# Two-layer encoder trunk: the order of products, SwiGLU transposes and token sums at the start of each FFN

## The chip, the core and the metric

The kernel runs on one core of one Trainium2 chip. The metric is the device time of one execution in microseconds (us); smaller is better. A kernel's time is the median of its runs. One further execution is taken with the hardware profiler; all rows below come from it. Engines are named as in the profile: PE (TensorE, matrix products), PEld (its weight loads), DVE (VectorE), ACT (ScalarE), POOL (GpSimd), SP (SyncE, which issues the DMAs).

## What is computed

A trunk of two layers over 256 tokens of width 1024, all in float32. Each layer is a half-step SwiGLU FFN, a token-mixing block and a second half-step FFN:

```python
def swiglu(h, w_up, w_down):
    a, b = jnp.split(h @ w_up, 2, axis=-1)
    return (jax.nn.silu(a) * b) @ w_down

for l in range(DEPTH):                      # 2
    h = rms_norm(x, ffn1_pre_g[l])
    x = x + 0.5 * rms_norm(swiglu(h, ffn1_w_up[l], ffn1_w_down[l]), ffn1_post_g[l])
    h = rms_norm(x, mix_pre_g[l])
    ...                                     # pooling, differential attention, cross-attention, gates
    x = x + rms_norm(merged @ w_out[l], mix_post_g[l])
    h = rms_norm(x, ffn2_pre_g[l])
    x = x + 0.5 * rms_norm(swiglu(h, ffn2_w_up[l], ffn2_w_down[l]), ffn2_post_g[l])
```

D_FF is 2816, so w_up is 1024 x 5632 and w_down 2816 x 1024. There are four FFNs in all.

## The kernel before

**Precision.** Every float32 operand of a product is split into a high part in the PE's fast format (ACT copies it, tiles `wh` for weights) and the remainder (DVE subtracts, `wl`). A product is three matrix products: high by high, high by low, low by high (`mm3`, L229). Weights come from memory in units of 128 x 2048 (`raw`, 1 MB, five buffers) and are split by `split_unit` (L113) into five pairs of `wh`/`wl` buffers; a sixth unit waits until the PE has done with the first.

**Tokens.** The 256 tokens are two halves c = 0 and 1 of 128 rows. The normed activations lie transposed and split in `xhl`. The hidden width is cut into 11 blocks p of 256 columns. The up product of block p and half c (`up`, L344) uses two weight units (upper and lower half of the 1024 inputs), has 24 matmuls of 512 columns, and fills one PSUM bank: 256 columns of a, 256 of b. Below it is called product pc: 00, 10, 01 and so on, the block first. `swiglu` (L334) then has ACT take the Silu of a into `sg` (L340) and DVE multiply by b into `hn` (L341), both SBUF tiles of the eight-buffer pool `s2`. Its result must be transposed for the down product: `turned` (L320) puts a closure on the list `pending`; when `flush` (L307) calls it, the PE makes two 128 x 128 transposes into a bank `mb` (L325), and ACT and DVE split that into `hid[p]` (L164, L165). Below the transposes of block p and half c are t00, t10 and so on.

**PSUM.** Eight banks: four accumulators `acc`, two `ma` for products, two `mb` for transposes. `down(p)` (L311) adds block p's down product into the four accumulators, which are taken at the first of them, `down(0)`, and kept to the FFN's end. The stage ahead uses the same four for its own result; `post_norm` (L217) reads them last.

**Start of an FFN.** The first FFN (the kernel's first stage) starts with `up_first` and is left out here. The three later ones make, in this order, products 00, 10, 01, 11 (L446 to L448), each in an `ma` bank, and after each product's matmuls `flush()` issues every transpose that is pending. So the PE's order is 00, 10, t00, 01, t10, 11, t01. The second half's normed tokens are only just being made when the FFN starts: their eight transposes (L207) are placed by hand after the 37th of these matmuls (`issue_after(late, done[T_UP])`, T_UP = 36), that is in the middle of product 10. ACT and DVE then split them into `xhl` (L164, L165), and ACT also copies them unsplit into four `s2` tiles, `kept` (L212). From these `token_sums` (L372) forms four sums and differences on DVE (L375 to L378) and splits each (ACT and DVE, L164 and L165) for the products of `group`.

**The rest of an FFN.** Blocks follow a list, `PLAN`: for the three later FFNs `u2 d0 g3 d1 d2 u5 d3 g6 d4 d5 u8 d6 g9 d7`. `u` is `up_both` (two products of one block), `d` is `down`, and `g` is `group` (L382), which makes two blocks at once by seven products of half the size from sums of weight units (DVE adds whole `raw` tiles, L364, then they are split like others) and sums of tokens. Its second product, into an `mb` bank, is the first that reads the token sums.

**Order on the engines.** A planner takes the instructions in program order as priority and lays out each engine's own order ahead of time, by what it expects to be ready; where its own estimate says that an operand is late, it takes later instructions first. Each engine then executes its list in order and waits where an operand is late.

Of the kernel before, what the change touches and what calls it, by code (L numbers as in the profile page):

```python
# [51 lines left out]
def encoder_kernel(ctx, tc, x_d, xt_d, mem_d, memt_d, pos_d, w_d, gains_d, cols_d, lamv_d, poolw_d, cst_d, out_d):  # L52
# [24 lines left out]
    def t2(shape=(P, 512), dt=F32):  # L77
        return s2.tile(list(shape), dt, name="s2")
# [48 lines left out]
    def next_unit():  # L127
        parts = 4 if fine[0] > 0 else 2
        fine[0] -= 1
        return split_unit(next_raw(), parts)  # L130
# [6 lines left out]
    def issue_after(late, early):  # L137
        for i in late:
            tc.add_manual_dep(i.ins, early.ins.name, mybir.DependencyInfo(mybir.DependencyClass.NoSync, mybir.DependencyReason.DATA),
                              reason="issue order")  # L140

    def in_order(ins):
        for early, late in zip(ins, ins[1:]):
            issue_after([late], early)
# [6 lines left out]
    def rstd_of(halves, fold=1.0, between=None, into=None, listed=False):  # L151
        s, sq = sm(2), []
        for i, h in enumerate(halves):
            junk = small.tile([P, 512], BF16, name="junk", bufs=2)
            sq.append(nc.scalar.activation(out=junk, in_=h, func=AF.Square, scale=fold / 32.0, accum_out=s[:, i:i + 1]))  # L155
        v = sm(1)
        var = nc.vector.tensor_scalar(out=v, in0=s[:, 0:1], scalar1=s[:, 1:2], scalar2=fold * fold * EPS, op0=ALU.add, op1=ALU.add)  # L157
        if between:
            between(var)
        r = rsqrt(v, 1, into)  # L160
        return (var, sq) if listed else r

    def split(ps, h, l):
        high = nc.scalar.copy(out=h, in_=ps)  # L164
        return high, nc.vector.tensor_tensor(out=l, in0=ps, in1=h.bitcast(F32), op=ALU.subtract)  # L165

    def halves(t):
        return [t[:, 0:512], t[:, 512:1024]]
# [95 lines left out]
    def form_b2(out, lo, hi, c, xx):  # L264
        return mm3(out, half_b(lo, 0, c, xx) + half_b(hi, 1, c, xx))
# [31 lines left out]
    def ffn(i, xx, late, kept, g_post, finish, ahead, raw_rstd=None):  # L297
# [9 lines left out]
        def flush(leave=0):  # L307
            while len(pending) > leave:
                pending.pop(0)()
# [24 lines left out]
        def swiglu(p, c, ps):  # L334
            sg, hn = t2((P, S)), t2((P, S))
            if raw_rstd:
                nc.scalar.activation(out=sg, in_=ps[:, 0:S], func=AF.Silu, scale=raw_rstd[c])
                nc.vector.scalar_tensor_tensor(out=hn, in0=ps[:, S:2 * S], scalar=raw_rstd[c], in1=sg, op0=ALU.mult, op1=ALU.mult)
            else:
                nc.scalar.activation(out=sg, in_=ps[:, 0:S], func=AF.Silu)  # L340
                nc.vector.tensor_tensor(out=hn, in0=ps[:, S:2 * S], in1=sg, op=ALU.mult)  # L341
            turned(hn, c, [p])

        def up(p, c, ws, bank=ma_bank):  # L344
            ps = bank()
            now = form_b2(ps, ws[0], ws[1], c, xx)
            flush()
            swiglu(p, c, ps)
            return now

        def up_both(p):
            ws = (next_unit(), next_unit())
            for c in range(2):
                up(p, c, ws)

        def product(out, at, w, first=True, last=True):
            wv = [t.rearrange("p (k m) -> p k m", k=4) for t in w]
# [14 lines left out]
        def token_sums():  # L372
            a11, a12, a21, a22 = (kept[c, b] for c in range(2) for b in range(2))
            s1 = t2()
            nc.vector.tensor_tensor(out=s1, in0=a22, in1=a21, op=ALU.subtract)  # L375
            nc.vector.tensor_tensor(out=a21, in0=a11, in1=a21, op=ALU.subtract)
            nc.vector.scalar_tensor_tensor(out=a11, in0=s1, scalar=-1.0, in1=a11, op0=ALU.mult, op1=ALU.subtract)
            nc.vector.scalar_tensor_tensor(out=a12, in0=a11, scalar=-1.0, in1=a12, op0=ALU.mult, op1=ALU.subtract)  # L378
            for j, t in enumerate((s1, a11, a21, a12)):
                split(t.rearrange("p (k t) -> p k t", t=P), sums[:, 0, 4 * j:4 * j + 4, :], sums[:, 1, 4 * j:4 * j + 4, :])  # L380
# [42 lines left out]
        def up_first(p, ws):  # L423
            banks = [ma_bank(), ma_bank()]
            for j, w in enumerate(ws):
                for c in range(2):
                    mm3(banks[c], half_b(w, j, c, xx), j == 0, j == 1)
            for c in range(2):
                swiglu(p, c, banks[c])

        if raw_rstd:
            ws = [(next_unit(), next_unit())]
            hs, ls = first_high, first_low
            (ha, la), (hb, lb), (hc, lc), (hd, ld) = (zip(*late[c, b]) for b in range(2) for c in range(2))
            in_order([*ha, *hs[0:4], *hb, *hc, hs[4], hs[5], *hd, *hs[6:8]])
            in_order([*la, *ls[0:4], *lb, *lc, ls[4], ls[5], *ld, *ls[6:8]])
            ws.append((next_unit(), next_unit()))
            for c in range(2):
                rstd_of(halves(x[c]), 1.0, None, raw_rstd[c])
            up_first(0, ws[0])  # L440
            for c in range(2):
                up(1, c, ws[1], acc_bank)
        else:
            ws = [(next_unit(), next_unit()) for _ in range(2)]
            done = []
            for c in range(2):  # L446
                for p in range(2):
                    done += up(p, c, ws[p])  # L448
            issue_after(late, done[T_UP])
            token_sums()  # L450
        for n, (what, p) in enumerate(PLAN[bool(kept)]):
            if what == "d":
                down(p)
            elif what == "u":
                up_both(p)
            else:
                group(p)
            if not kept and n == 5:
                ahead()
# [403 lines left out]
    kept = None  # L863
    for i, (kind, l, row) in enumerate(stages):
        nx = {}

        def finish(c):
            if i + 1 == len(stages):
                for b in range(2):
                    fs = slice(b * 512, (b + 1) * 512)  # L870
                    nc.sync.dma_start(out=out_d[c * P:(c + 1) * P, fs], in_=x[c][:, fs])
                return []
            if c == 0:
                nx["xx"] = xt_pair()
                nx["kept"] = {} if stages[i + 1][0] == "ffn" else None
                nx["g"] = gain(stages[i + 1][1] * 10 + stages[i + 1][2])
            return pre_norm(c, halves(x[c]), nx["g"], nx["xx"], nx["kept"])()

        if kind == "ffn":
            def ahead():  # L880
                if i == 0:
                    setup()
                    mem_scale()
                if row == 0:
                    nx["mem"] = mem_gain(l)

            late = ffn(i, cur, late, kept, gain(l * 10 + row + 1), finish, ahead, [rst[:, c:c + 1] for c in range(2)] if i == 0 else None)
        else:
            late = mix(l, cur, late, mem, finish)
        cur, mem, kept = nx.get("xx"), nx.get("mem"), nx.get("kept")  # L890
# [117 lines left out]
```

## Time and profile before

| | us |
|---|---|
| median of 3 runs | 1126.62 |
| the runs | 1125.84, 1126.62, 1129.25 |
| the profiled execution, device time | 1127.05 |
| its span, first to last instruction | 1124.9 |
| PE busy | 1109.0 (99%) |
| DVE busy | 893.5 (79%) |
| ACT busy | 651.9 (58%) |
| granted PE clock, mean | 0.997 |

The profiled execution's device time is 2.15 us over its span, and 0.43 us over the median. A granted clock of 1.00 is 2.4 GHz, of 0.50 is 1.2 GHz. The three FFNs in question start at about 385, 566 and 940 us of the span. A matmul's row in a timeline shows a modelled duration, which overlaps with the next one's start; how often matmuls start tells the PE's real pace.

### The profile page before, as it was taken

How to read it: one execution, taken by the hardware profiler on the slowest of the kernel's cores; microseconds unless marked ns; L12 is line 12 of the kernel's file. 1: busy time of each engine (PE TensorE's matmuls, PEld its weight loads, DVE VectorE, ACT ScalarE, POOL GpSimd, SP SyncE). 2: the span in 40 equal slices, each digit the busy share in tenths (PEclk: the TensorE clock that was granted, in tenths of full speed). 3: DMA queues.
4: the chain of work that ended last, by engine and by line, in shares of the span. 5: the costliest groups of instructions: out<-in, count | busy, mean ns of one | idle time of the engine just before them, and what ended most of it. 6: DMA issues, size and time to landing. Idle time of an engine off the chain costs nothing.

```text
span 1124.9 us, 13897 instructions
## 1 busy us (share of the span) xinstructions
PE 1109.0 (99%) x5247; PEld 913.2 (81%) x5247; DVE 893.5 (79%) x1215; ACT 651.9 (58%) x1082; POOL 26.1 (2%) x37
## 2 busy tenths in 40 slices
PE   9999999999999999999999999999999999999997
PEld 6888888888888878888878888878887887888886
DVE  6767456657758889999989999995776687999994
ACT  7657355556575557475575664755566546574561
POOL 0000000000000100000000000010000001000000
PEclk9999999999999999999999999999999999999999
DMA  9965643554553554573851835666455634263831
GB/s 342 388 229 225 219 152 117 192 220 150 206 206 132 195 179 148 190 264 136 310 190 73 299 135 202 219 240 218 160 175 191 244 149 169 75 245 135 293 112 38
DMA packets 35489, 218.27 MB, mean 194 GB/s; under 512 B 4192, under 2 KB 4448, under 8 KB 11232
## 3 DMA queue, kind: packets, MB, share of 16 engines
q1 hardware_dynamic: 35424, 217.40, 53.4%
q8 instruction: 41, 0.67, 0.2%
q14 instruction: 24, 0.20, 0.1%
HBM read 216.33 MB, written 1.05 MB: 193 GB/s over the span
## 4 chain that ended last, share of the span: by engine, by line
PE 92%; DVE 4%; ACT 1%; DMA 1%; POOL 1%; issue 0%; SPq 0%; DVEq 0%; POOLq 0%; ACTq 0%
PE ma L235 52%; PE acc L277 23%; PE mb L235 8%; DVE wl L120 2%; PE acc L235 2%; PE mb L325 2%; POOL sm L148 1%; PE acc L663 1%; DMA hid<-in_memt 1%; PE acc L686 1%; PE mb L563 1%; DVE x L227 1%; DMA raw<-in_w 1%; PE acc L749 1%; ACT wh L119 0%; PE mb L207 0%
## 5 line engine op out<-in xcount | busy, mean ns | idle before, releaser
L120 DVE TENSOR_TENSOR wl<-raw,wh 128x1024 fp32r<-128x1024 f32 (+1 forms) x498 | 524.2, 1092 | 101.6 <-ACT wh L119 99.0
L235 PE MATMUL ma<-wh,xhl 128*128 128x512 f32 x1760 | 562.3, 394 | 1.1 <-ACT wh L119 1.1
L119 ACT CAST wh<-raw 128x1024 fp32r<-128x1024 f32 (+1 forms) x498 | 445.0, 948 | 197.9 <-PE ma L235 65.6
L235 PEld LDWEIGHTS ma<-wh,xhl 128*128 128x128 f32 x1760 | 330.3, 188 | 70.8 <-ACT wh L119 2.4
L235 PE MATMUL ma<-wl,xhl 128*128 128x512 f32 x880 | 346.3, 394 | 0.5 <-DVE wl L120 0.5
L277 PE MATMUL acc<-wh,hid 128*128 128x512 f32 x704 | 228.2, 395 | 0.0
L235 PEld LDWEIGHTS ma<-wl,xhl 128*128 128x128 f32 x880 | 165.8, 188 | 35.0 <-DVE wl L120 1.5
L277 PEld LDWEIGHTS acc<-wh,hid 128*128 128x128 f32 x704 | 132.2, 188 | 26.8
L277 PE MATMUL acc<-wl,hid 128*128 128x512 f32 x352 | 137.1, 391 | 0.0
L235 PE MATMUL mb<-wh,xhl 128*128 128x512 f32 x280 | 90.5, 389 | 0.0
L364 DVE TENSOR_TENSOR raw<-raw 128x2048 f32<-128x2048 f32 x36 | 82.4, 2288 | 0.4
L277 PEld LDWEIGHTS acc<-wl,hid 128*128 128x128 f32 x352 | 66.3, 188 | 12.7
L235 PEld LDWEIGHTS mb<-wh,xhl 128*128 128x128 f32 x280 | 52.6, 188 | 11.0
L340 ACT ACTIVATE s<-ma 128x256 f32<-128x256 f32 x30 | 11.2, 386 | 77.1 <-PE ma L235 77.1
L235 PE MATMUL mb<-wl,xhl 128*128 128x512 f32 x140 | 54.5, 389 | 0.0
L148 POOL TENSOR_TENSOR sm<-sm,mhalf 128x1 f32<-128x1 f32 (+1 forms) x26 | 23.2, 891 | 1009.8 <-DVE sm L157 830.3
L164 ACT CAST hid<-mb 128x256 fp32r<-128x256 f32 x88 | 32.5, 369 | 16.2 <-PE mb L325 13.3
L165 DVE TENSOR_TENSOR hid<-mb,hid 128x256 fp32r<-128x256 f32 x88 | 37.0, 420 | 5.4 <-ACT hid L164 5.0
L277 PE MATMUL acc<-wh,xhl 128*128 128x512 f32 x128 | 40.7, 394 | 0.0
L155 ACT ACTIVATE junk<-acc 128x512 bf16<-128x512 f32 x24 | 14.3, 597 | 43.7 <-PE acc L277 43.7
L325 PE MATMUL mb<-ident,s 128*128 128x128 f32 x176 | 30.7, 273 | 5.3 <-DVE s L341 5.3
L325 PEld LDWEIGHTS mb<-ident,s 128*128 128x128 f32 x176 | 23.1, 140 | 15.5 <-issue 6.5
(159 smaller groups left out, 832.9 us busy)
## 6 DMA issues: line engine op xcount, KB each, us to landing
raw<-in_w SPq DMA_DIRECT2D x189, 1024.0 KB, 4.9
gain<-in_gains SPq DMA_DIRECT2D x17, 512.0 KB, 4.7
raw<-in_w SPq DMA_DIRECT2D x8, 256.0 KB, 6.4
hid<-in_memt SPq DMA_DIRECT2D x8, 256.0 KB, 6.6
hid<-in_xt SPq DMA_DIRECT2D x4, 256.0 KB, 6.0
raw<-in_w SPq DMA_DIRECT2D x2, 512.0 KB, 6.3
x<-in_x SPq DMA_DIRECT2D x4, 256.0 KB, 6.7
hid<-in_mem SPq DMA_DIRECT2D x4, 256.0 KB, 7.3
```

The costliest lines, as they stand in the source:

```text
L119: high = nc.scalar.copy(out=h[:, cs], in_=raw[:, cs])
L120: low = nc.vector.tensor_tensor(out=l[:, cs], in0=raw[:, cs], in1=h.bitcast(F32)[:, cs], op=ALU.subtract)
L148: nc.gpsimd.tensor_tensor(out=r, in0=v, in1=mhalf[:, :n], op=ALU.pow)
L155: sq.append(nc.scalar.activation(out=junk, in_=h, func=AF.Square, scale=fold / 32.0, accum_out=s[:, i:i + 1]))
L164: high = nc.scalar.copy(out=h, in_=ps)
L165: return high, nc.vector.tensor_tensor(out=l, in0=ps, in1=h.bitcast(F32), op=ALU.subtract)
L227: nc.vector.scalar_tensor_tensor(out=x[c][:, fs], in0=ts[b], scalar=r, in1=x[c][:, fs], op0=ALU.mult, op1=ALU.add)
L235: done.append(nc.tensor.matmul(out=out, lhsT=lhsT, rhs=rhs, start=(first and i == 0), stop=(last and i == n - 1)))
L277: done.append(nc.tensor.matmul(out=banks[b], lhsT=a, rhs=ww[:, k, fs], start=(kk == first and k == 0 and i == 0), stop=(kk == last and k = ...
L325: nc.tensor.transpose(out=tp[:, u * P:(u + 1) * P], in_=hn[:, u * P:(u + 1) * P], identity=ident)
L364: nc.vector.tensor_tensor(out=out, in0=a, in1=b, op=ALU.add)
L563: ins.append(nc.tensor.transpose(out=tp[:, i * P:(i + 1) * P], in_=a[:, hh, kt * P:(kt + 1) * P], identity=ident))
```

## The change

`up` gets a bank function and a number of closures to leave pending. At the start of the three later FFNs all four products are issued with two closures left, and half 1 (01 and 11) goes to two accumulator banks in place of the `ma` banks. So t00 is issued after product 11. `up_both` leaves one closure pending at its first half and none at its second. `token_sums`, which stood after the four products, is called in block 2's `up_both`, between products 20 and 21. The order on the PE becomes 00, 10, 01, 11, t00, 20, t10, t01, 21, t11, t20, then `down(0)`.

In the first FFN, `up_both(2)` leaves t11 until after product 21; its other steps are as before. In all later `up_both` calls the list is empty at the call, and the order is as before.

```diff
-        def up(p, c, ws, bank=ma_bank):
+        def up(p, c, ws, bank=ma_bank, leave=0):
             ps = bank()
             now = form_b2(ps, ws[0], ws[1], c, xx)
-            flush()
+            flush(leave)
             swiglu(p, c, ps)
             return now
 
         def up_both(p):
             ws = (next_unit(), next_unit())
             for c in range(2):
-                up(p, c, ws)
+                up(p, c, ws, leave=1 - c)
+                if kept and p == 2 and c == 0:
+                    token_sums()
...
             for c in range(2):
                 for p in range(2):
-                    done += up(p, c, ws[p])
+                    done += up(p, c, ws[p], acc_bank if c else ma_bank, 2)
             issue_after(late, done[T_UP])
-            token_sums()
```

## Rows read from the trace of the kernel before

**Rows 1.** The page: busy time of each engine; the chain that ended last.
```profile
PE 1109.0 (99%) x5247; PEld 913.2 (81%) x5247; DVE 893.5 (79%) x1215; ACT 651.9 (58%) x1082; POOL 26.1 (2%) x37
...
PE 92%; DVE 4%; ACT 1%; DMA 1%; POOL 1%; issue 0%; SPq 0%; DVEq 0%; POOLq 0%; ACTq 0%
```

**Rows 2.** PE's waits: us in total, times, longest us.
```profile
PE mb L325 <- DVE s L341: 5.3, 3, 2.0
```

**Rows 3.** PE's timeline at t00 in three FFNs: start us, us, instruction [idle before].
```profile
396.23 0.39 PE L235 MATMUL ma<-wl,xhl 128*128 128x512 f32 x1
396.46 0.39 PE L235 MATMUL ma<-wh,xhl 128*128 128x512 f32 x1
398.79 0.41 PE L325 MATMUL mb<-ident,s 128*128 128x128 f32 x2 [1.95 <-DVE s L341]
...
579.06 0.41 PE L325 MATMUL mb<-ident,s 128*128 128x128 f32 x2 [1.41 <-DVE s L341]
...
950.90 0.41 PE L325 MATMUL mb<-ident,s 128*128 128x128 f32 x2 [1.99 <-DVE s L341]
```

**Rows 4.** ACT's and DVE's timelines ahead of the first of these stalls.
```profile
393.94 1.07 ACT L164 CAST xhl<-mb 128x512 fp32r<-128x512 f32 x2 [1.56 <-PE mb L207]
396.55 1.18 ACT L212 COPY s<-mb 128x512 f32<-128x512 f32 x2 [1.53 <-DVE xhl L165]
397.63 0.67 ACT L340 ACTIVATE s<-ma 128x256 f32<-128x256 f32 x2
...
386.29 0.68 DVE L222 TENSOR_TENSOR s<-acc,gain 128x512 f32<-128x512 f32 x1
...
395.82 1.29 DVE L165 TENSOR_TENSOR xhl<-mb,xhl 128x512 fp32r<-128x512 f32 x2
397.02 1.29 DVE L120 TENSOR_TENSOR wl<-raw,wh 128x512 fp32r<-128x512 f32 x2
398.22 0.76 DVE L341 TENSOR_TENSOR s<-ma,s 128x256 f32<-128x256 f32 x2
```

**Rows 5.** Stretches: us, busy time (and instructions) of each engine, granted clock, DMA.
```profile
402.00:570.00 168.00, 168.00 (x765) 138.78 (x765) 159.79 (x180) 103.86 (x150) 1.96 (x3) 1.00 0.54 196
...
951.60:955.20 3.60, 3.60 (x10) 2.80 (x9) 0.43 (x1) 0.12 (x1) 0.00 (x0) 0.53 0.68 271
```

**Rows 6.** Chain of waits in order of time, product 01: start us, us, what.
```profile
399.20 5.50 PE ma L235 x24
...
951.32 7.07 PE ma L235 x24
```

**Rows 7.** ACT's and DVE's timelines from product 01 to the first group.
```profile
402.01 2.00 ACT L119 CAST wh<-raw 128x1024 fp32r<-128x1024 f32 x2 [2.40 <-PE ma L235]
...
403.10 2.36 DVE L120 TENSOR_TENSOR wl<-raw,wh 128x1024 fp32r<-128x1024 f32 x2 [3.03 <-ACT wh L119]
...
406.37 4.77 DVE L120 TENSOR_TENSOR wl<-raw,wh 128x1024 fp32r<-128x1024 f32 x4 [0.24 <-ACT wh L119]
411.06 0.42 DVE L341 TENSOR_TENSOR s<-ma,s 128x256 f32<-128x256 f32 x1
...
411.72 0.68 DVE L375 TENSOR_TENSOR s<-s,s 128x512 f32<-128x512 f32 x1
412.32 2.29 DVE L364 TENSOR_TENSOR raw<-raw 128x2048 f32<-128x2048 f32 x1
...
418.80 0.68 DVE L165 TENSOR_TENSOR xhl<-s,xhl 128x512 fp32r<-128x512 f32 x1
...
427.94 1.23 DVE L120 TENSOR_TENSOR wl<-raw,wh 128x1024 fp32r<-128x1024 f32 x1 [1.12 <-ACT wh L119]
```

**Rows 8.** DVE's and PE's timelines in the first group and the down product behind it.
```profile
430.29 0.39 PE L235 MATMUL mb<-wh,xhl 128*128 128x512 f32 x1
...
446.43 1.22 DVE L120 TENSOR_TENSOR wl<-raw,wh 128x1024 fp32r<-128x1024 f32 x1
...
447.87 0.48 PE L277 MATMUL acc<-wl,hid 128*128 128x512 f32 x1
```

## Prediction

> **What bounds the kernel now.** I read the page first. PE is busy for 1109.0 of 1124.9 us, and 92% of the chain that ended last is PE's [rows 1]. So the end comes earlier only if PE's instructions become fewer or start closer together. The change takes none away: the same matmuls and transposes are issued in another order. What it can win is PE's idle time, 15.9 us in the span.
>
> PE's waits come next. The longest entry is the one that the change aims at: transposes (L325) that wait for the SwiGLU multiplication on DVE (L341), 5.3 us in three waits, the longest 2.0 [rows 2]. PE's timeline shows one at the start of each later FFN, at t00: 1.95, 1.41 and 1.99 us [rows 3]. The first FFN has none. These rows understate the loss. Matmuls start 0.23 us apart while a row's modelled duration is 0.39 [rows 3], so 0.16 us of each stall is covered by the modelled end. The loss is 2.11, 1.57 and 2.15, together 5.8 us.
>
> Why t00 is late is in the timelines of ACT and DVE [rows 4]. Product 00 was complete a whole product (5.50 us [rows 6] and eight transposes) before 10 ended, but its Silu stands in ACT's list behind the work for the second half's tokens: ACT splits them at 393.94, then waits 1.53 us for DVE's part of that split before it makes the unsplit copies at 396.55, and begins the Silus of 00 and 10 at 397.63. DVE multiplies from 398.22, PE transposes at 398.79. Product 01, which needs neither, stands behind t00 on PE. It could not have started at once even so: its bank `ma` is product 00's, and that is read last by the multiplication at 398.22, which ends near 398.6.
>
> **The change, part by part.**
>
> **Later t00.** With t00 behind product 11, the matmuls of 01 can follow 10 at 396.69 (396.46 plus the spacing of 0.23). Their inputs are there: DVE's first half of the token split, which begins at 395.82 and lasts some 0.65, is needed at the third matmul (397.1), its second half, done at 397.1, at the fifteenth (399.9) [rows 4]. The multiplications of 00 and 10, done by 399.0, now have until about 407.8, two products later (24 matmuls last 5.50 [rows 6]). Deferring t00 alone, with the `ma` bank kept, would move the start of 01 only from 398.96 to about 398.7.
>
> **Accumulator banks for 01 and 11.** That is what removes the second wait. The stage ahead reads the last of its accumulators at 386.29 to 386.97 [rows 4], ten microseconds before 01 wants one. `down(0)` wants all four back after product 21, when the multiplication of 11 is about two products old. No cost, and the two parts together remove the stall: -5.8 us in three FFNs.
>
> **Clock.** Product 01 takes 5.50 us in one FFN and 7.07 in the last [rows 6]. The granted clock from 951.60 to 955.20 is 0.53, between the two levels because nearly the whole stretch is at 1.2 GHz [rows 5]. It fell right behind the 1.99 us stall, and rose during the product. Behind the stall of 1.95 us at 396.85 it did not fall: from 402 to 570 it is 1.00 [rows 5], and product 01 there has its 5.50. Without the stall I expect no fall: -1.57 us against this profiled execution. The Trainium skill (TensorE: Matmul & The Clock Gate, "The HAM clock gate (the 'warmup' mystery)") says that the moment at which the clock changes varies from run to run, because the gate's window does not start with the kernel. By that a fall behind such a stall is chance, other executions of the old kernel lack it or have several, and one would not book it: the sum would be 1122.4 in place of 1120.8. The three rows, one fall for three stalls, agree.
>
> **Transposes in pairs.** t10 and t01 now follow each other, as do t11 and t20. Their number stays, both `mb` banks are there, and each bank is wanted again a whole product (5.5 us) later, while a split on DVE takes 0.42 and comes one to two microseconds after the transposes. 0, with a bound of 0.1 us either way.
>
> **Token sums.** No DMA and no POOL instruction moves with them, only eight on DVE and four on ACT. They run at present from 411.72, right behind the multiplication of 11 (411.06), to 419.48 [rows 7], and the first product that reads them starts at 430.29 [rows 8]: 10.8 us to spare. Their first tile is taken from the pool after `hn` of product 20 now, so they start one product later, near 414.3 in the new order's time, and end by about 422 to 424. The new start of that product is 2.1 us earlier, 428.2. At least 4 us remain; no wait. On pool `s2`: four copies, `hn` of 00, 10 and 01 and a `sg` fill all eight tiles, and `hn` of 11 takes the tile of 00 when t00 is done, a few tenths after product 11. That delays no one whom PE waits for.
>
> **What is late next.** DVE. From 403.10 to 427 it has 0.24 us idle, then 1.12 [rows 7], and over the rest of this FFN it is busy 159.79 of 168 us [rows 5]. In the first group its splits end just in time: `wl` of the unit behind the group is begun at 446.43 and done at 447.65; PE reads it at 447.87 [rows 8], 0.22 us later. So PE keeps its gain only as far as DVE gets earlier too. DVE's busy stretch begins where PE frees a weight buffer: ACT waits 2.40 us for PE, splits at 402.01, and DVE, idle for 3.03 us, follows at 403.10 [rows 7]. PE frees it in the middle of 01, so this start moves by the same 2.1 us. Against that stand two items. The splits of t00 and t10 (0.42 each) lay in or before DVE's idle time and now fall into the busy stretch: 0.8. And between the multiplications of 11 and 20, 5.7 us apart, the token sums are missing. Ready in their place are one raw add (2.29) and the split of its unit (2.36), 4.65 together [rows 7], so up to 1.1 us of new idle time. DVE is late by 0.8 to 1.9 us relative to PE's new times. The margin takes 0.2, and the present idle 1.12 at 427.94, which ends with an add that can now come earlier, may take another 1.1. PE thus loses 0 to 1.7 us in each of three FFNs. I take 0.4, near the lower end, since the list of a planner fills such holes with whatever is ready: +1.2 us, with bounds of 0 and +5.1.
>
> **First FFN.** Its t11 goes behind product 21; block 1's down product is a whole block later. 0.
>
> **Sum.** From the profiled execution's 1127.05: 1127.05 - 5.8 - 1.57 + 1.2 = 1120.9, which I round down to 1120.8. That execution lies 0.43 us over the median of its runs, which I leave, as the fall of the clock explains it.
>
> **Rivals.**
>
> **DVE becomes the bound.** The gain at t00 is given back in the first group: PE waits for `wl` (L120) there. For it: the margin of 0.22 us and DVE's full stretches. Against it: that stretch starts on PE's release. At the upper bound, 1.7 us in each FFN, 1127.05 - 5.8 - 1.57 + 5.1 = 1124.8. The Trainium skill (TensorE: Matmul & The Clock Gate, its table of specifications) calls ACT's and DVE's queues strict FIFO. By that the later token sums, once begun, hold back every split listed behind them; rows 4, where the Silu waits behind the copies, agree.
>
> **It does not do what it says.** The planner could lay PE's list out as before, for instance with t00 ahead of 11. Against it: 01 and 11 are ready and have priority. Part of the stall would remain: 1125 to 1127.
>
> **Slower.** The place is the stretch on DVE between the multiplications of 11 and 20, where the token sums are missing. If the planner puts nothing in their place, because it takes the next units for not yet loaded or their buffers for not yet free, DVE idles there for all 5.7 us. With the two splits DVE is then 6.5 us late, of which the margin and the present idle time take 1.3; PE loses 5.2 in each first group: 1127.05 - 5.8 - 1.57 + 3 x 5.2 = 1135.3. It decides against the change where the loss per FFN is over (5.8 + 1.57) / 3 = 2.5 us, that is from 3.0 us of new idle time on DVE. Against it: in the old order the group's first raw add runs at 412.32, right behind the first token sum [rows 7], so these units are loaded by then.
>
> **How the numbers follow.** About 0.3%, 3.4 us, is what a measurement here can tell from no change; the borders are 1123.2 and 1130.0. Forecast, 1119.5 to 1122.4: 0.66. DVE as bound, 1122.4 to 1126: 0.19, of which 0.05 is below 1123.2. Not done: 0.07. Slower: 0.08. Faster 0.71, same 0.21, slower 0.08. The range reaches from the full gain without any loss (1119.7), less 1 us for the spread of the runs, to the upper bound of DVE's price with the clock's fall half kept (1125.5).
>
> **What would show it.** In the new profile PE's wait for L341 at L325 is gone from the three FFNs, and the matmul before t00 writes `acc`. Product 01 starts within 0.3 us of 10's end, the clock is 1.00 up to the last microseconds, and product 01 lasts 5.5 us in the last FFN. The first group starts about 2 us earlier after the FFN's start. Wrong would be new PE waits for DVE wl L120 or ACT wh L119 in the first groups, a wait at the first `mb` product, or idle time on DVE ahead of the token sums of over 2 us.

## The result, and the profile after

The changed kernel takes 1118.93 us (median of 6 runs, 1118.06 to 1119.85) against 1126.95 for the kernel before (6 runs, 1125.84 to 1129.25). The ratio is 0.9929, 95% interval 0.9918 to 0.9940: 8.0 us less. The forecast was 1120.8, in a range from 1118.7 to 1125.5. The profiled execution has a span of 1116.0 us and a device time of 1118.06, against 1124.9 and 1127.05. Two executions of the experiments below, 1590.01 us with three extra multiplications and 1875.72 with six, ran at granted clocks of 0.655 and 0.556 and count in none of the times and ratios.

The page of the changed kernel answers to [rows 1] (lines of `kernel.py` that stand behind `up` are numbered up to two higher than in the kernel before):

```profile
PE 1106.6 (99%) x5247; PEld 912.6 (82%) x5247; DVE 892.5 (80%) x1215; ACT 651.6 (58%) x1082; POOL 25.5 (2%) x37
PE 95%; DMA 2%; ACT 1%; DVE 1%; POOL 0%; issue 0%; SPq 0%; DVEq 0%; POOLq 0%; ACTq 0%
```

PE's longest waits over the whole span, to be held against [rows 2] (us in total, times, longest us):

```profile
PE acc L861 <- DVE s L858: 1.2, 1, 1.2
PE mb L207 <- DVE s L199: 0.7, 1, 0.7
```

The instructions are as many as before. The wait for L341 is gone, DVE's share of the chain has fallen from 4% to 1%, and of PE's two longest waits one lies in the first microseconds and the other at the transposes near 740 us. The remaining ones, of 0.2 to 0.4 us, make 1.0 us together and lie outside the three later FFNs.

The chain of waits at the start of the second FFN answers to the first line of [rows 6] (start us, us, what). From 384.95 on it holds nothing but PE; from the transposes of the second half's tokens on it reads:

```profile
392.66 0.87 PE mb L207 x8
393.53 2.51 PE ma L235 x11
396.04 10.88 PE acc L235 x48
406.92 0.22 PE mb L325 x2
407.14 5.48 PE ma L235 x24
412.62 0.44 PE mb L325 x4
413.06 5.45 PE ma L235 x24
418.51 0.44 PE mb L325 x4
418.95 1.16 PE acc L277 x5
```

Products 01 and 11 run as one piece of 10.88 us in accumulator banks, t00 follows, and then come 20, two transposes twice, 21 and so on. The same piece lasts 10.88 us in the last FFN, where product 01 alone had 7.07 [rows 6].

A good measure of the change is the stretch from the first of the eight transposes of the second half's tokens (L207) to the first matmul of `down(0)` (L277). PE's timeline gives both ends. In the second and the last FFN of the kernel before, and then of the changed kernel, these are:

```profile
393.31 1.03 PE L207 MATMUL mb<-ident,s 128*128 128x128 f32 x8
421.75 0.47 PE L277 MATMUL acc<-wh,hid 128*128 128x512 f32 x1
...
945.38 1.03 PE L207 MATMUL mb<-ident,s 128*128 128x128 f32 x8
975.44 0.47 PE L277 MATMUL acc<-wh,hid 128*128 128x512 f32 x1
```

```profile
392.50 1.04 PE L207 MATMUL mb<-ident,s 128*128 128x128 f32 x8
418.70 0.48 PE L277 MATMUL acc<-wh,hid 128*128 128x512 f32 x1
...
940.35 1.03 PE L207 MATMUL mb<-ident,s 128*128 128x128 f32 x8
966.55 0.48 PE L277 MATMUL acc<-wh,hid 128*128 128x512 f32 x1
```

| stretch L207 to `down(0)`, us | FFN 2 | FFN 3 | FFN 4 |
|---|---|---|---|
| before | 28.44 | 27.92 | 30.06 |
| changed | 26.20 | 26.21 | 26.20 |
| difference | 2.24 | 1.71 | 3.86 |

The three stretches have become equal, and the sum of the differences is 7.8 us. The spans differ by 8.9. Of the other 1.1 us, 0.8 was won before the second FFN began and 0.3 at the transposes near 740 us. Both are places where executions differ anyhow: `down(0)` of the first FFN starts between 42.06 and 43.25 us in ten profiles with the same or nearly the same code there, and PE waits between 0.74 and 1.88 us at the transposes near 740.

DVE's timeline answers to [rows 7]:

```profile
399.88 2.36 DVE L120 TENSOR_TENSOR wl<-raw,wh 128x1024 fp32r<-128x1024 f32 x2 [1.72 <-ACT wh L119]
402.16 0.42 DVE L341 TENSOR_TENSOR s<-acc,s 128x256 f32<-128x256 f32 x1
402.87 4.82 DVE L120 TENSOR_TENSOR wl<-raw,wh 128x1024 fp32r<-128x1024 f32 x4 [0.29 <-ACT wh L119]
407.60 0.42 DVE L341 TENSOR_TENSOR s<-acc,s 128x256 f32<-128x256 f32 x1
407.94 0.41 DVE L165 TENSOR_TENSOR hid<-mb,hid 128x256 fp32r<-128x256 f32 x1
408.27 4.61 DVE L366 TENSOR_TENSOR raw<-raw 128x2048 f32<-128x2048 f32 x2
...
414.93 0.68 DVE L377 TENSOR_TENSOR s<-s,s 128x512 f32<-128x512 f32 x1
...
420.75 0.68 DVE L165 TENSOR_TENSOR xhl<-s,xhl 128x512 fp32r<-128x512 f32 x1
...
425.40 1.23 DVE L120 TENSOR_TENSOR wl<-raw,wh 128x1024 fp32r<-128x1024 f32 x1 [1.11 <-ACT wh L119]
```

The hole between the multiplications of 11 (407.60) and 20 (414.59) holds two raw adds, 4.61 us, where I had counted on one. The token sums run from 414.93 to 421.43. The stage began 0.81 us earlier in this execution; with that taken off, the split at 425.40 comes 1.7 us earlier than the one at 427.94 did [rows 7], and PE's first `mb` product, at 427.26, is 2.2 us earlier than 430.29 [rows 8]. So DVE did fall 0.5 us behind PE there. It catches up inside the group. The same DVE work, from that split to the one at 444.69 of the kernel before and its answer at 441.75, takes 17.97 us there and 17.57 now. The changed kernel's busy time in that stretch (us, then PE, PEld, DVE, ACT and POOL with the number of instructions, then the granted clock, the DMA share and GB/s):

```profile
425.40:442.97 17.57, 17.57 (x79) 14.52 (x78) 17.57 (x19) 13.70 (x17) 0.00 (x0) 1.00 0.47 160
```

DVE is busy for all of it, where before it waited 0.30 us for a PE product. The last of these splits now ends at 442.97, and PE reads it at 443.35; before it was 445.91 and 446.38. DVE is 0.1 us behind in the end, and PE has no wait. At the split for which the prediction gave a margin of 0.22 us (446.43 [rows 8]) the margin has even grown: it now begins at 443.49, is done at 444.71, and PE reads it at 445.16. But within this stretch DVE has no idle time left with which it could catch up any further.

### The profile page after: what moved, and what is told of

Read it like the earlier page. It is cut to its first block, busy times and chain, and to the rows that moved or that the text cites. A ratio compares the mean times of both kernels' runs of the same rounds, so it can differ in the third digit from the quotient of the medians.

```text
span 1116.0 us, 13913 instructions
## 1 busy us (share of the span) xinstructions
PE 1106.6 (99%) x5247; PEld 912.6 (82%) x5247; DVE 892.5 (80%) x1215; ACT 651.6 (58%) x1082; POOL 25.5 (2%) x37
## 4 chain that ended last, share of the span: by engine, by line
PE 95%; DMA 2%; ACT 1%; DVE 1%; POOL 0%; issue 0%; SPq 0%; DVEq 0%; POOLq 0%; ACTq 0%
PE ma L235 52%; PE acc L277 24%; PE mb L235 9%; PE acc L235 5%; PE mb L325 2%; PE mb L207 1%; PE acc L664 1%; PE acc L687 1%; PE mb L564 1%; DMA hid<-in_memt 1%; DMA hid<-in_xt 1%; PE acc L750 1%; DMA raw<-in_w 0%; POOL sm L148 0%; PE acc L734 0%; DVE wl L120 0%
## 5 line engine op out<-in xcount | busy, mean ns | idle before, releaser
L235 PE MATMUL ma<-wh,xhl 128*128 128x512 f32 x1664 | 530.1, 393 | 0.1
L235 PEld LDWEIGHTS ma<-wh,xhl 128*128 128x128 f32 x1664 | 311.7, 188 | 65.5 <-issue 1.7
L235 PE MATMUL ma<-wl,xhl 128*128 128x512 f32 x832 | 327.1, 393 | 0.4 <-DVE wl L120 0.2
L277 PE MATMUL acc<-wh,hid 128*128 128x512 f32 x704 | 227.8, 395 | 0.0
L235 PEld LDWEIGHTS ma<-wl,xhl 128*128 128x128 f32 x832 | 156.4, 188 | 33.0 <-DVE wl L120 1.3
L277 PEld LDWEIGHTS acc<-wh,hid 128*128 128x128 f32 x704 | 132.2, 188 | 26.9
L277 PE MATMUL acc<-wl,hid 128*128 128x512 f32 x352 | 136.8, 390 | 0.0
L235 PE MATMUL mb<-wh,xhl 128*128 128x512 f32 x280 | 90.5, 389 | 0.0
L277 PEld LDWEIGHTS acc<-wl,hid 128*128 128x128 f32 x352 | 66.3, 188 | 12.7
L235 PEld LDWEIGHTS mb<-wh,xhl 128*128 128x128 f32 x280 | 52.6, 188 | 10.9
L235 PE MATMUL mb<-wl,xhl 128*128 128x512 f32 x140 | 54.5, 389 | 0.0
L235 PE MATMUL acc<-wh,xhl 128*128 128x512 f32 x160 | 51.6, 391 | 0.0
L340 ACT ACTIVATE s<-ma 128x256 f32<-128x256 f32 x24 | 8.9, 386 | 65.6 <-PE ma L235 65.2
L277 PE MATMUL acc<-wh,xhl 128*128 128x512 f32 x128 | 40.7, 394 | 0.0
L235 PEld LDWEIGHTS acc<-wh,xhl 128*128 128x128 f32 x160 | 30.0, 188 | 6.2
```

The lines of the kernel that those rows point to most:

```text
L235: done.append(nc.tensor.matmul(out=out, lhsT=lhsT, rhs=rhs, start=(first and i == 0), stop=(last and i == n - 1)))
L277: done.append(nc.tensor.matmul(out=banks[b], lhsT=a, rhs=ww[:, k, fs], start=(kk == first and k == 0 and i == 0), stop=(kk == last and k = ...
```

## The experiments

All ratios are to the kernel before, of runs on the same chip (its median there is 1127.0 to 1127.6 us). The stretch L207 to `down(0)` is given where it tells something.

**The banks alone.** Kernel before, half 1 in accumulator banks:

```diff
-                    done += up(p, c, ws[p])
+                    done += up(p, c, ws[p], acc_bank if c else ma_bank)
```

> The kernel before, with half 1 (01, 11) in accumulator banks, and nothing else. Theory (both parts are needed; t00 stands in front of 01 on PE): PE still waits for L341 at t00 in the three later FFNs, 1.4 to 2.0 us each by the rows, so the time stays within 1 us of before, 1126 to 1128. Rival (the bank alone is what held 01): the stalls shrink to under 0.5 us and the time falls by 4 us or more, to under 1123.

Measured: 1121.30 us, ratio 0.9940 (0.9925 to 0.9955). Three quarters of the gain come from one argument. My theory is refuted as it stood, and the rival holds for the most part: L341 still ends three waits, but of 0.6 us. PE's timeline shows why:

```profile
396.77 0.39 PE L235 MATMUL ma<-wh,xhl 128*128 128x512 f32 x1
397.00 0.39 PE L235 MATMUL acc<-wh,xhl 128*128 128x512 f32 x1
397.23 0.39 PE L235 MATMUL acc<-wl,xhl 128*128 128x512 f32 x1
397.45 0.62 PE L235 MATMUL acc<-wh,xhl 128*128 128x512 f32 x2
397.91 0.39 PE L235 MATMUL acc<-wl,xhl 128*128 128x512 f32 x1
398.13 0.39 PE L235 MATMUL acc<-wh,xhl 128*128 128x512 f32 x1
399.11 0.41 PE L325 MATMUL mb<-ident,s 128*128 128x128 f32 x2 [0.59 <-DVE s L341]
```

Once 01 has a free bank, six of its matmuls stand in front of t00 on PE, though t00 comes first in the program. So the planner, by its rule, did not take t00 for ready and went around it; that what is left of the wait is what its estimate missed is my reading, not shown. The stretches are 27.09, 27.02 and 27.14 us: 0.8 to 0.9 over the changed kernel's.

**The deferral alone.** Changed kernel, 01 and 11 back in `ma` banks:

```diff
-                    done += up(p, c, ws[p], acc_bank if c else ma_bank, 2)
+                    done += up(p, c, ws[p], ma_bank, 2)
```

> The changed kernel with 01 and 11 back in ma banks; transposes left pending and later token sums stay. Theory (01's bank is freed by the multiplication of 00): product 01 waits on PE for L341 where t00 did, 0.2 to 0.3 us shorter each, so the time is 1126 to 1127.5 and PE's waits name ma L235 <- DVE s L341, about 5 us in three. Rival (the place of t00 alone matters): no such wait, the time is that of the changed kernel, 1118 to 1120.

Measured: 1127.08 us, ratio 0.9998 (0.9987 to 1.0008). As the theory had it, nothing is won, though the two longest waits are no shorter than before. PE's wait has moved from t00 to product 01:

```profile
PE ma L235 <- DVE s L341: 4.8, 3, 2.0
```

PE's timeline at the first and the third of these waits:

```profile
395.96 0.39 PE L235 MATMUL ma<-wh,xhl 128*128 128x512 f32 x1
398.30 0.47 PE L235 MATMUL ma<-wh,xhl 128*128 128x512 f32 x1 [1.96 <-DVE s L341]
...
951.28 0.47 PE L235 MATMUL ma<-wh,xhl 128*128 128x512 f32 x1 [1.99 <-DVE s L341]
```

Stretches of the same execution; the granted clock is the third figure from the end, before the DMA share and GB/s:

```profile
399.30:402.90 3.60, 3.60 (x10) 2.85 (x9) 0.00 (x0) 0.00 (x0) 0.00 (x0) 0.53 0.78 291
952.20:955.90 3.70, 3.70 (x11) 2.86 (x10) 0.00 (x0) 0.00 (x1) 0.00 (x0) 0.54 0.70 263
960.00:1100.00 140.00, 140.00 (x637) 115.67 (x636) 135.71 (x142) 84.19 (x110) 0.00 (x0) 1.00 0.48 173
```

Both waits of 2.0 us were followed by a stretch nearly all at 1.2 GHz (0.53 and 0.54); the one of 0.9 in between was not. The stretches L207 to `down(0)` are 30.07, 27.39 and 30.07 us.

**Token sums at their old place.** Changed kernel, `token_sums()` behind the four products again:

```diff
-                if kept and p == 2 and c == 0:
-                    token_sums()
...
             issue_after(late, done[T_UP])
+            token_sums()
```

> The changed kernel with the token sums back behind the four products. Theory (the sums have over 5 us to spare in either place, and DVE fills the hole with raw adds and splits): within 0.5 us of the changed kernel, 1118.4 to 1119.4. Rival A (the later sums are themselves a gain, because the adds and splits they made room for reach PE earlier): 1.5 us or more slower than the changed kernel, with PE waits in the first groups. Rival B (the later sums cost DVE time): 1 us or more faster.

Measured: 1118.88 us, ratio 0.9919 (0.9905 to 0.9934), stretches 26.21 us three times. The sums' place has no price in either direction that could be seen here. The theory holds, both rivals fall.

**One closure left pending in place of two.**

```diff
-                    done += up(p, c, ws[p], acc_bank if c else ma_bank, 2)
+                    done += up(p, c, ws[p], acc_bank if c else ma_bank, 1)
```

> The changed kernel with one closure left pending in the four products in place of two: t00 comes behind 01, t10 behind 11. Theory (t00's multiplication ends near 398.2 in the changed kernel's time, and 01 ends at 401.3): no wait at t00 and the whole gain stays, within 0.5 us of the changed kernel. Rival (the second product is needed, because DVE's list is late again at t10 or t01): waits for L341 at L325 come back, over 1 us in sum, and the time is 1120 or more.

Measured: 1119.74 us, ratio 0.9922 (0.9906 to 0.9939), stretches 26.25 us, and no wait for L341. The median is 0.8 us above the changed kernel's, over the 0.5 I allowed, but the ratios' intervals cover each other and the profile shows longer waits outside the later FFNs: 1.3 us for `wh` in the first microseconds, where the changed kernel has none, and 1.6 at the transposes near 741, where it has 0.7. One product of delay is enough.

**All transposes after product 20.** Changed kernel, `up_both` without its new argument:

```diff
-                up(p, c, ws, leave=1 - c)
+                up(p, c, ws)
```

> The changed kernel, but block 2's first product issues all that is pending: t10, t01 and t11 follow product 20 in a row, t20 follows 21. Only two mb banks exist, so t11 needs the bank of t10, which ACT and DVE read last. Theory (as the run with the banks alone showed, the planner fills such a wait with matmuls of the next product): under 0.5 us per FFN, total 1118.4 to 1120.4. Rival (PE waits for the split of t10, cast 0.37 and subtraction 0.42 behind other work, 1 to 2 us in each FFN): 1122 to 1125, with waits at L325 for DVE L165.

Measured: 1118.52 us, ratio 0.9923 (0.9906 to 0.9939), stretches 26.23 us. No wait for a bank appears. The change in `up_both` is not needed for the gain.

**Without the unsplit copies.** This goes at the cause: kernel before, ACT's copies of the second half left out.

```diff
-                    keep[c, b] = t2()
-                    nc.scalar.copy(out=keep[c, b], in_=ps)
+                    keep[c, b] = keep[0, b] if c else t2()
+                    if c == 0:
+                        nc.scalar.copy(out=keep[c, b], in_=ps)
```

> The kernel before without ACT's unsplit copies of the second half's tokens (L212 for c = 1): the token sums then use the first half's copies in their place, so that part of the computation is wrong. All else as before, t00 in front of 01 included. Theory (the Silu of 00 is late because it stands behind these copies, which wait for DVE's part of the token split): the stall at t00 falls from 2.1, 1.6, 2.1 us to 1.0 or less each, and the time to 1121 to 1124. Rival (DVE is late by itself, with the token and weight splits in front of the multiplication): the stalls stay at 1.4 us or more, the time at 1125.5 or more.

Measured: 1119.53 us, ratio 0.9934 (0.9919 to 0.9949), stretches 26.29 us. The stall is gone, not only smaller, with t00 still in front of 01 and the banks as before. DVE's load is unchanged (892.9 us busy, 893.5 before), so its load alone is not the cause: it was the copies. But they act through DVE's list too. The multiplication of 00 now runs at 395.03, ahead of the token split, where it stood behind that split and two weight splits [rows 4].

**Silu before the copies.** Nothing left out; the two copies are emitted behind product 00 and its SwiGLU:

```diff
-                    nc.scalar.copy(out=keep[c, b], in_=ps)
+                    if c == 0:
+                        nc.scalar.copy(out=keep[c, b], in_=ps)
+                    else:
+                        keep.setdefault("copies", []).append((keep[c, b], ps))
...
                     done += up(p, c, ws[p])
+                    if (p, c) == (0, 0):
+                        for out, src in kept.pop("copies"):
+                            nc.scalar.copy(out=out, in_=src)
```

> The kernel before with ACT's unsplit copies of the second half's tokens put behind product 00 and its SwiGLU in program order, and nothing left out; PE's order of products and transposes as before. Theory (the copies in front of the Silu are the cause, and the run without them lost the whole stall): the Silu of 00 starts at 395 to 396, the stalls at t00 fall to under 1 us each, though t00 still has to wait for the bank that the copies read; time 1120 to 1123. Rival (the planner puts the copies first anyway, or the bank that t00 needs is now the late one): stalls of 1.4 us or more, 1125.5 to 1128.

Measured: 1119.86 us, ratio 0.9934 (0.9918 to 0.9951). The timelines of ACT, DVE and PE (line numbers from L235 on are three higher here):

```profile
390.87 0.37 ACT L343 ACTIVATE s<-ma 128x256 f32<-128x256 f32 x1
...
393.57 1.29 DVE L120 TENSOR_TENSOR wl<-raw,wh 128x512 fp32r<-128x512 f32 x2
394.77 0.42 DVE L344 TENSOR_TENSOR s<-ma,s 128x256 f32<-128x256 f32 x1
...
395.71 1.28 DVE L165 TENSOR_TENSOR xhl<-mb,xhl 128x512 fp32r<-128x512 f32 x2
...
396.58 0.39 PE L238 MATMUL ma<-wh,xhl 128*128 128x512 f32 x1
397.07 0.44 PE L328 MATMUL mb<-ident,s 128*128 128x128 f32 x2
```

The Silu of 00 runs at 390.87, where I had expected 395 to 396, and its multiplication at 394.77, 3.5 us earlier than in [rows 4] and ahead of the token split. t00 starts 0.27 us late, of which the modelled end of the matmul before it covers 0.16. The stretches are 26.64, 26.37 and 26.64 us. It is even better than the theory said. A change in the program order on ACT, with PE's order and the banks untouched, takes away nearly all of the stall too.

What moved with it is the order on DVE, and that half of the mechanism the prediction does not have. In the kernel before, the multiplication waits for the Silu in only one of the three FFNs, and there for 0.34 us:

```profile
578.49 0.76 DVE L341 TENSOR_TENSOR s<-ma,s 128x256 f32<-128x256 f32 x2 [0.34 <-ACT s L340]
...
950.33 0.76 DVE L341 TENSOR_TENSOR s<-ma,s 128x256 f32<-128x256 f32 x2
```

In the other two, DVE comes to it without a gap from the token split and two weight splits (395.82 and 397.02 in [rows 4]). There a Silu that only ran earlier, with DVE's list as it was, would have saved nothing. The copies cost what they do because the planner, with the Silu behind them, also lays the multiplication behind these splits. That this is its estimate at work follows from its rule; the runs show that the multiplication moves when the copies do.

**More work on DVE.** Changed kernel, with three or six extra multiplications (128 x 512) behind that of product 11, in each later FFN:

```diff
-                nc.vector.tensor_tensor(out=hn, in0=ps[:, S:2 * S], in1=sg, op=ALU.mult)
+                last_mult[0] = nc.vector.tensor_tensor(out=hn, in0=ps[:, S:2 * S], in1=sg, op=ALU.mult)
...
             issue_after(late, done[T_UP])
+            prev = last_mult[0]
+            for _ in range(3):                       # 6 in the second of the two
+                junk = small.tile([P, 512], BF16, name="junk", bufs=2)
+                more = nc.vector.tensor_tensor(out=junk, in0=x[0][:, 0:512], in1=x[0][:, 512:1024], op=ALU.mult)
+                issue_after([more], prev)
+                prev = more
```

> The changed kernel with three more DVE multiplications of 128x512 (about 0.6 us apart, 1.8 us) behind the multiplication of product 11 in each of the three later FFNs, into an unused tile. Theory (DVE is the next bound; 0.2 us of margin in the first group and 1.1 us of idle time before it): PE waits 0.3 to 0.7 us for wl L120 or wh L119 in each first group, total 1119.5 to 1121. Rival (the planner's fillers and five weight buffers leave more slack): no new wait, within 0.5 us of the changed kernel.

> As the run before with six multiplications (3.6 us). Theory (DVE is the next bound): each us beyond 1.3 is paid on PE, 2.0 to 2.6 us in each FFN, total 1124.5 to 1127. Rival (slack of several us): within 1 us of the changed kernel, 1118 to 1120.

Measured: 1128.44 us with three (median of nine), ratio 1.0010 (0.9998 to 1.0022), and 1134.82 with six (median of three), ratio 1.0064 (1.0046 to 1.0082). Both lie well above what I expected. The whole gain is lost with 1.9 us of DVE work per FFN. The stretches to `down(0)` keep their 26.21 us; the loss is in the first group. The timelines of DVE and PE with three:

```profile
408.95 1.89 DVE L456 TENSOR_TENSOR junk<-x 128x512 bf16<-128x512 f32 x3
...
439.95 0.61 PE L235 MATMUL mb<-wh,xhl 128*128 128x512 f32 x2
441.22 0.50 PE L235 MATMUL ma<-wh,xhl 128*128 128x512 f32 x1 [0.65 <-ACT wh L119]
442.99 0.51 PE L235 MATMUL mb<-wl,xhl 128*128 128x512 f32 x1 [1.27 <-DVE wl L120]
```

and the clock behind it (third figure from the end):

```profile
443.90:447.60 3.70, 3.70 (x11) 2.88 (x10) 3.64 (x5) 3.70 (x5) 0.00 (x0) 0.54 0.95 368
```

Starts are late by 0.81 us at 441.22 and 1.55 at 442.99 (gaps of 1.04 and 1.77 against some 0.23 between starts), 2.36 together for 1.89 us of added work, and the same two waits stand in the other two FFNs. That DVE's work is the next bound is borne out by the two waits, for wl and wh as expected; my price for it was far too low. The 2.36 us are not the price of the added work alone, though. The planner has laid out another order in the group: the raw add that runs at 434.29 in the changed kernel, ahead of the add for an `ma` product, runs at 437.72 here, behind that add.

**The first FFN too.** Changed kernel, `up(1, c, ws[1], acc_bank, 2)` in place of `up(1, c, ws[1], acc_bank)` in the first FFN.

> The changed kernel with the same deferral in the first FFN: block 1's two products leave two closures pending, so PE does not meet t01 in the middle of product 10, where the changed kernel's profile shows a wait of 0.4 us for L338. Theory (PE's only wait there is that one): 0.3 to 0.6 us faster than the changed kernel, 1118.3 to 1118.7, hardly to be told from it. Rival (the first FFN is bound by the arrival of weights, so a wait that is removed returns as a wait for wh or wl): no difference.

Measured: 1120.53 us, ratio 0.9941 (0.9928 to 0.9955). Not faster. The wait for L338 is gone, and PE waits there for a weight unit instead:

```profile
25.90 0.73 PE L235 MATMUL acc<-wh,xhl 128*128 128x512 f32 x2 [1.03 <-ACT wh L119]
```

That fits the rival. Whether it is 1 us slower or only had later weights is open: this part differs between executions by as much, and the wait at the transposes near 740 was 1.88 us in this execution against 0.74.

## Why the prediction was right

**Where the stall comes from** was right in its root, and the two runs on the copies show it: ACT's Silu of 00 behind two copies that wait for DVE. The prediction takes the Silu for the step that made the multiplication late. The rows show that only in one of three FFNs; in the others the multiplication's own place, behind the token split and two weight splits on DVE, ended last, and the copies worked through the planner's order. The price does not depend on this.

**Its price, 5.8 us, and the clock's, 1.57.** Together 7.4 us; the three stretches became shorter by 7.8. The row sum holds within 0.4 us: 0.13 to 0.14 us in each FFN, whose source stays open. The steps that gave it, the modelled ends (0.16 us each) and the start of 01 right at 10's end, are seen in the chain. On the clock, more profiles now speak: of five single waits of PE of 1.4 to 2.0 us in the kernel before and in the deferral alone (1.95, 1.41 and 1.99 [rows 3]; 1.96 and 1.99), three were followed by some 3.6 us at 1.2 GHz, all of them among the four of 1.95 or more. None of the profiles without these waits or the added DVE work has a fall between 20 and 1110 us. So it belongs in the sum, as a share, and was not peculiar to that one execution. The 35 executions of the kernel before that stand beside the experiments say the same: ten with a mean granted clock of 0.994 took 1128.9 us on average, ten with 0.997 took 1126.5, and three with 0.999 took 1125.7. By these figures some had more falls than the profiled one (0.997) and some fewer. The Trainium skill (TensorE: Matmul & The Clock Gate, "The HAM clock gate (the 'warmup' mystery)") says that the moment at which the clock changes varies from run to run. What the runs here show is that whether it falls varies: of two waits of 1.95 and 1.96 us, one had no fall behind it and one had.

**"Accumulator banks ... the two parts together remove the stall"** was right in its sum and wrong in its shares. That deferral alone brings nothing was predicted to a few tenths. That the banks alone would bring little I only wrote in the expectation of the first run, and it fell. The step that failed there is the assumption that PE's order is the program's. The prediction lets a planner fill holes on DVE with whatever is ready, and does not do so on PE.

**What is late next** is the term that was mis-sized: +1.2 us, measured 0. The items behind it were there in part: two splits more lie in the busy stretch, and DVE was 0.5 us behind PE's new times at the first group. But the hole was filled with two raw adds instead of one. The idle time ahead of the group, which I had thought might shrink, is still there (1.11 us after 1.12). The 0.5 us were made good where DVE had idled inside the group. I had counted the margin at one place and not the idle time behind it. This term explains most of the distance between the forecast, 1120.8, and 1118.93. The rest, 0.7 us, is of the size of what was won above 7.4 (0.4) and of the starts and transposes that vary.

**DVE as the bound** did not come true, and is still the right rival: 1.89 us more DVE work in the same place gives it, with PE's waits at the wl and wh named. In the order that the planner then chose, the slack is less than 1.89 us; how much there is in the changed kernel's own order the run does not show. What I had expected it to cost (0.3 to 0.7 us in each FFN) was too low: three times 2.36 and one fall of the clock make 8.7, and the medians are 9.5 apart. The price left out that the planner orders the group anew and that such a wait can lower the clock.

**Token sums, transposes in pairs, first FFN**: 0 fits each of them. The run with the sums at the old place shows it for the first, the run with all transposes after 20 for the second. That run also has the old order in the first FFN, where `down(0)` starts at 42.27 us, inside the spread given above. The change in `up_both`, which leaves t11 until after 21, is unneeded in any FFN.

## What to carry to other kernels

When PE waits for a short step on another engine, look first at what stands ahead of that step in that engine's list, and in the list of the engine that feeds it: here two copies that nobody needed soon, waiting themselves, cost 7 to 8 us, and moving them was worth nearly as much as a new order of products on PE. A free bank for the next product is what let the planner go around a late operand here; deferral without the bank only moved the wait. And before adding work to an engine that shows 95% in a stage, test its slack with a dummy of known length: 1.9 us per FFN took this whole gain away. Then look whether the order around the dummy stayed the same.

## What the runs showed of the hardware

A single wait of PE of 2.0 us was enough, in three of four cases (the kernel before and the deferral alone), for some 3.6 us at 1.2 GHz behind it. That cost another 1.6 us, nearly as much as the wait itself: product 01 took 7.07 us instead of 5.50 [rows 6]. In the same two profiles waits of 0.9 and 1.4 us had none behind them. Nor had waits of 1.60 and 1.88 us at the transposes near 740 (one closure left pending, first FFN too). In the first 12 us of the span, however, where PE had started its first matmul at 1.19 us, waits of 1.33, 1.64 and 2.12 us for `wh` (one closure left pending, without the copies, the banks alone) were each followed by a fall. So the length of the wait alone does not decide. With three multiplications added on DVE, a wait of 0.65 us and one of 1.27 that ended 1.8 us later stood in each of the three FFNs, and in one of them a fall followed.
